# Hybrid encoder layer: strips of eight key columns, token order changed at the bank reads, six second-stage units by seven products

## The chip, the cores and the metric

The kernel runs on one core of a Trainium2 chip. The metric is the device time of one execution in microseconds (us). A core has a matrix engine (TensorE, PE in the profile; PEld are its weight loads), a vector engine (VectorE, DVE), a scalar engine (ScalarE, ACT), GpSimd (POOL) and SyncE (SP), which here issues nearly all DMA transfers. Each engine works through its own queue in order and waits for the others by semaphores. PSUM has eight banks of 512 fp32 words a partition; matmuls write there, DVE and ACT read it.

## The reference

One layer of an encoder trunk over 2048 tokens (a grid of 32 rows by 64 columns) of width 1024, 16 heads of 64, all fp32. With `DEPTH = 1` only the neighbourhood mixer runs:

```
h = rmsnorm(x, norm_0)
q, k, v, gate = split(h @ w_in_0, 4)
s = q.k / 8 + rpb          # 8 rows x 16 columns of keys around each query
o = softmax(s) @ v
x = x + (o * silu(gate)) @ w_out_0
y = rmsnorm(x, norm_f)
```

A query at row r and column c sees the 8 rows and 16 columns of the grid that lie around it, moved inwards at the border.

## The kernel before

**Numbers.** A product of fp32 matrices is made of three matmuls: every operand is split into a high part (`h`, an ACT copy that rounds to fp32r) and a low part (`l`, a DVE subtraction), and h.h, h.l and l.h are added in PSUM. Each split therefore costs one ACT and one DVE instruction.

**Units and stages.** The columns of q, k and gate (g) are made in units of 256 columns (two head pairs `p`); `(k, 0)` to `(k, 3)` are the four units of k. Tokens come in four chunks `c` of 512. `stage_one` (lines 546 to 753) makes chunks 0 and 1 of v and then of all twelve units; `stage_two` (756 to 866) makes chunks 2 and 3 of v and of the units in `units_two`, which are k, q and g of j=0. The nine units that are left are made for chunks 2 and 3 by `projections` (868), matmul by matmul between the attention steps.

**Seven products.** In both stages a unit (256 columns by two chunks) is made by `seven_products` (378), a Strassen-Winograd scheme: 7 block products of 12 matmuls, 84 in all, where `projections` takes 96. For that DVE makes four sums of weight quarters (`sum_`, line 400), ACT and DVE split seven weight forms (393, 394), and the products gather in three banks: products 1 and 2 share one, 6, 7 and 4 one, 5 and 3 one. Between products that share a bank the partial result is read: `keep` (ACT, 418) after product 1, `add` (DVE, 422) after 6 and after 7, `out_` (DVE, 428) after 5, 4 and 3, `evac` (DVE, 313 or 315) after 2. In stage one the results are also multiplied by the tokens' rstd `rb[c]` (POOL, 430). `give` (321) turns a finished tile into what is stored: for k a high and a low part (341, 342), for g a gate by tanh (328, 329), for q the tile itself. It is stored to DRAM some matmuls later by `store` (288), which keeps a list by a clock that counts matmuls.

**Token order of before.** x, k, v and g are in grid order (row, column). q is put into tiles when a bank is read: `tiled` and `blocked` (280, 283) order the 8 rows by 64 columns of a chunk as four blocks C of 8 rows by 16 columns, in runs of 16 words. Attention handles one token block T (8 rows) of a head pair p in two steps, with two blocks C each. The keys of (T, C) are a rectangle of `KEY_ROWS[T]` by `KEY_COLS[C]`: 11 to 15 rows, 24 or 32 columns. For the product with v they are cut by `blocks` (61) into groups of four rows by the full width, 96 or 128 keys, the last one with three rows. v has to have the same order: `evac_v` (365) stores it to `vd`, `copy_v` (942) copies it in DRAM to `vc`, once per (p, C, half), with the four rows beside each other, and `load_v` (932) loads one tile per (p, T, C).

**The attention steps.** The loop at 1337 runs through 64 pairs `i` = (p, T, two blocks C), first all p for T=0, then T=1 and 2, then T=3. A step issues loads and the bias tables of the next block (`begin`; `bias`, POOL, 970), then feeds matmuls of the remaining units, later of the output product, to PE (`feed`: an allowance `amount[i]` of 22 a step, and 19.7 in the last 18), then `normalise(i-1)` (DVE 1004, POOL 1006), `turns(i-2)`, `scores(i)` and `values(i-2)`. `scores` makes s in four banks (988), adds bias and mask while it takes the row maximum (DVE 995), and takes exp (ACT 998). `turns` transposes the weights on PE (1011) and brings them to SBUF, one half of the queries by DVE (1036), the other by ACT (1035, with another instruction for a group of three rows). `values` multiplies by v (1056), and after the second step of a block DVE multiplies by the gate (1070).

**The end of a row.** The output product (1250 to 1254), residual and final norm follow in `outputs`; `finish` (1169) puts the root (eight tiny DVE instructions), the scaling and the store of a tile of 128 rows on the list, 12, 24 and 44 matmuls later.

Of the kernel before, what the change touches and what calls it, by code (L numbers as in the profile page):

```python
# [10 lines left out]
F32 = mybir.dt.float32  # L11
# [12 lines left out]
NP = H // 2  # L24
# [19 lines left out]
def mask_table():  # L44
    out = []
    for t, (u0, u1) in enumerate(TYPE_ROWS):
        T = (0, 1, 3)[t]
        for c, (v0, v1) in enumerate(TYPE_COLS):
            C = (0, 1, 3)[c]
            qr = T * 8 + np.arange(8)[:, None, None, None]  # L50
            qc = C * 16 + np.arange(16)[None, :, None, None]
            kr = T * 8 + np.arange(u0, u1)[None, None, :, None]
            kc = C * 16 + np.arange(v0, v1)[None, None, None, :]
# [17 lines left out]
def build(ctx, tc, x, xr, xt, wg, rpb, w_out, n0, nf, masks, out):  # L71
# [7 lines left out]
    vd = [dram.tile([4, 4, GW, 8, 128], F32, name=f"vd{u}") for u in range(2)]  # L79
    vc = {(p, C): dram.tile([4 * (c1 - c0), 8, 128], F32, name=f"vc{p}_{C}")  # L80
          for p in range(NP) for C, (c0, c1) in enumerate(KEY_COLS)}
# [12 lines left out]
    vp = pool("vp", 4)  # L94
# [114 lines left out]
    def spread_rstd(c):  # L209
        p = bank(512, "prb")  # L210
        h, l = dgs.pop(c)
        nc.tensor.matmul(p, onesr, h, start=True, stop=False)
        nc.tensor.matmul(p, onesr, l, start=False, stop=True)
        rb[c] = rbp([128, 512], F32, "rb")
        nc.scalar.activation(rb[c], p, AF.Copy)
# [5 lines left out]
    units_two = [(k, j) for j in range(1) for k in "kqg"]  # L221
    halves = [(k, j, 1, c) for j in range(1, 4) for g in (("k", "q", "g") if j < 3 else ("k", "qg")) for c in (2, 3) for k in g]
# [57 lines left out]
    def tiled(t):  # L280
        return t.rearrange("p (r C c) -> p C r c", r=8, c=16)

    def blocked(t):
        return t.rearrange("p (C r c) -> p C r c", r=8, c=16)
# [24 lines left out]
    def evac(kind, hp, c, p, then=None):  # L309
        state["event"] = clock[0]  # L310
        tmp = ev([128, 512], F32, "tmp")
        if kind != "q":
            nc.vector.tensor_tensor(tmp, p, rb[c], OP.mult)
        else:
            nc.vector.tensor_tensor(blocked(tmp), tiled(p), tiled(rb[c]), OP.mult)
        if then is None:
            give(kind, hp, c, tmp)
        else:
            then.append(lambda: give(kind, hp, c, tmp))

    def give(kind, hp, c, t, psum=False):
# [3 lines left out]
        written.add((kind, hp, c))  # L325
        if kind == "g":
            sg = ev([128, 512], F32, "sg")
            nc.scalar.activation(sg, t, AF.Tanh, scale=0.5)
            nc.vector.scalar_tensor_tensor(sg, sg, 1.0, t, op0=OP.add, op1=OP.mult)
            store(("g", hp, c), 12, lambda: nc.sync.dma_start(sgd[hp][:, s], sg))  # L330
            return
        if kind == "q":
            if psum:
                o = ev([128, 512], F32, "q")
                nc.scalar.activation(blocked(o), tiled(t), AF.Copy)
                t = o
# [4 lines left out]
        nc.scalar.activation(hi, t, AF.Copy)  # L341
        nc.vector.tensor_tensor(lo, t, hi.bitcast(F32), OP.subtract)
# [22 lines left out]
    def evac_v(u, t, p):  # L365
        v = ev([128, 512], F32, "v")
        nc.scalar.activation(v, p, AF.Copy, scale=rt[:, t:t + 1] if t < 8 else 1.0)
        dst = vd[u].rearrange("h r c g d -> g (r c) h d")[t // 2, t % 2 * 128:t % 2 * 128 + 128]
# [9 lines left out]
    def seven_products(us, c0, X1, also):  # L378
# [37 lines left out]
        def keep(n):  # L416
            U[n, 1] = ep([128, 512], F32, "p1")
            nc.scalar.activation(U[n, 1], B[n, 1], AF.Copy)

        def add(n, i, P):  # L420
            U[n, i] = xp([128, 512], F32, "u")
            nc.vector.tensor_tensor(U[n, i], B[n, P], U[n, 1], OP.add)  # L422

        def out_(n, a, c, P, u, then):
            kind, j = us[n]
            tmp = ev([128, 512], F32, "tmp")
            lay, of = (blocked, tiled) if kind == "q" else (lambda t: t, lambda t: t)
# [968 lines left out]
```

## Time and profile before

| | |
|---|---|
| time, median of 3 runs (lowest to highest) | 1084.95 us (1084.85 to 1085.42) |
| the profiled execution: time / span | 1086.36 us / 1084.5 us |
| busy PE / DVE / ACT / POOL | 1071.1 / 703.2 / 531.2 / 357.9 us |
| granted TensorE clock | 0.999 |
| DMA: bytes, mean rate | 231.90 MB, 214 GB/s |

Lines of the profile are named by the line of kernel.py (L411 is line 411). A busy PE means that some matmul is under way; matmuls overlap, so their durations add up to more than the time that they take. The stages lie at 1.8 to 96.7 us (v of stage one), 96.7 to 326.7 (twelve units), 326.7 to 414.2 (v of stage two), 414.2 to 471.2 (three units), and from there the attention steps, with the tail of the output product from 1028.

### The profile page before, as it was taken

The numbers are of one execution on the slowest core, as the hardware profiler recorded it, in microseconds if no ns is written. First come the engines' busy times: TensorE is split into PE (matmuls) and PEld (weight loads), VectorE is DVE, ScalarE is ACT, GpSimd is POOL, SyncE is SP. The second block draws the span as 40 slices with busy tenths as digits, with TensorE's granted clock in tenths as the row PEclk, the third lists the DMA queues.
The fourth block names the chain that finished last, engine by engine and source line by source line (L and its number), as shares of the span: only waits on it lengthen the run. The fifth ranks groups of instructions, "written<-read, shape, count | busy, mean of one in ns | idle before, by whom it ended". The sixth has DMA issues, their size and how long they took to land.

```text
span 1084.5 us, 21929 instructions
## 1 busy us (share of the span) xinstructions
PE 1071.1 (99%) x7657; PEld 877.1 (81%) x7657; DVE 703.2 (65%) x1644; ACT 531.2 (49%) x1345; POOL 357.9 (33%) x474
## 2 busy tenths in 40 slices
PE   9999999999999999999999999999999999999997
PEld 6888888888888888887888888888888787888885
DVE  5376778778997535576555555664676786776643
ACT  7545334333434334346555555564576565665431
POOL 0000222312221000017545534444447656566200
PEclk9999999999999999999999999999999999999999
DMA  9633557574764366889868876886899787887442
GB/s 313 212 97 106 202 173 210 163 232 146 256 188 143 108 172 170 258 277 310 245 205 267 253 216 204 255 269 200 246 319 294 230 268 231 274 262 226 126 149 78
DMA packets 145901, 231.90 MB, mean 214 GB/s; under 512 B 13824, under 2 KB 61184, under 8 KB 145792
## 3 DMA queue, kind: packets, MB, share of 16 engines
q1 hardware_dynamic: 145648, 230.25, 68.2%
q8 instruction: 61, 1.00, 0.4%
q14 instruction: 48, 0.39, 0.1%
q10 hardware_dynamic: 144, 0.26, 0.1%
HBM read 171.73 MB, written 73.40 MB: 226 GB/s over the span
## 4 chain that ended last, share of the span: by engine, by line
PE 92%; DVE 3%; DMA 1%; ACT 1%; issue 1%; SPq 0%; POOL 0%; ACTq 0%; DVEq 0%; POOLq 0%
PE pp L411 23%; PE pv L531 16%; PE o L1056 8%; PE s L988 6%; PE pp L359 6%; PE pp L357 6%; PE pp L355 6%; PE po L1254 6%; PE po L1252 5%; PE po L1250 5%; PE ph L1011 5%; PE zp L1269 1%; DMA k_hi<-hi 1%; DMA land<-in_xt_dram 0%; DVE f L394 0%
## 5 line engine op out<-in xcount | busy, mean ns | idle before, releaser
L1006 POOL TENSOR_SCALAR x<-x,st 128x360 f32<-128x360 f32 (+5 forms) x256 | 143.0, 578 | 235.0 <-DVE st L1004 192.3
L970 POOL TENSOR_TENSOR em<-e,mk 128x480 f32<-128x480 f32 (+5 forms) x160 | 136.3, 886 | 138.3 <-DMA raw<-in_xt_dram 135.0
L998 ACT ACTIVATE x<-x,st 128x360 f32<-128x360 f32 (+5 forms) x256 | 151.8, 595 | 44.4 <-DVE st L995 44.4
L411 PE MATMUL pp<-h,f 128*128 128x512 f32 x480 | 155.4, 389 | 0.0
L430 POOL TENSOR_TENSOR tmp<-tmp,rb 128x512 f32<-128x512 f32 x36 | 58.9, 1637 | 270.6 <-DVE tmp L428 223.7
L411 PE MATMUL pp<-t,f 128*128 128x512 f32 x540 | 130.0, 390 | 0.3 <-DVE u L422 0.2
L995 DVE CUSTOM_DVE_ANT_0 x<-s,em 128x360 f32<-128x360 f32 (+5 forms) x256 | 124.0, 539 | 5.3 <-PE s L988 1.4
L411 PEld LDWEIGHTS pp<-t,f 128*128 128x128 f32 x540 | 101.2, 188 | 22.2 <-DVE u L422 1.2
L359 PE MATMUL pp<-h,w 128*128 128x512 f32 x288 | 115.1, 400 | 0.0
L357 PE MATMUL pp<-l,w 128*128 128x512 f32 x288 | 113.2, 393 | 0.0
L355 PE MATMUL pp<-h,w 128*128 128x512 f32 x288 | 113.1, 393 | 0.0
L1035 ACT ACTIVATE pta<-ph 96x256 f32<-96x256 f32 (+1 forms) x224 | 58.5, 333 | 104.3 <-PE ph L1011 104.3
L1036 DVE COPY pta<-ph 128x384 f32<-128x384 f32 (+3 forms) x128 | 60.7, 514 | 72.7 <-PE ph L1011 72.5
L411 PEld LDWEIGHTS pp<-h,f 128*128 128x128 f32 x480 | 90.1, 188 | 18.8
L1254 PE MATMUL po<-wol,gh 128*128 128x512 f32 x252 | 100.3, 398 | 0.0
L1252 PE MATMUL po<-woh,gl 128*128 128x512 f32 x252 | 98.9, 393 | 0.0
L1250 PE MATMUL po<-woh,gh 128*128 128x512 f32 x252 | 98.9, 392 | 0.0
L1056 PEld LDWEIGHTS o<-pta,vt 96*64 96x64 f32 (+2 forms) x1792 | 83.6, 137 | 17.2 <-issue 10.2
L1056 PE MATMUL o<-pta,vt 96*64 96x128 f32 (+4 forms) x1792 | 92.3, 254 | 1.4 <-DVE pta L1036 1.0
L411 PE MATMUL pp<-l,f 128*128 128x512 f32 x240 | 93.4, 389 | 0.0
L531 PE MATMUL pv<-wh,h 128*128 128x512 f32 x256 | 88.1, 390 | 0.0
L531 PE MATMUL pv<-wh,l 128*128 128x512 f32 x256 | 88.0, 389 | 0.0
(148 smaller groups left out, 1916.6 us busy)
## 6 DMA issues: line engine op xcount, KB each, us to landing
raw<-in_wg_dram SPq DMA_DIRECT2D x126, 256.0 KB, 5.1
e<-in_rpb_dram SPq DMA_DIRECT2D x54, 240.0 KB, 3.9
vt<-vc SPq DMA_DIRECT2D x64, 192.0 KB, 3.7
row<-in_xr_dram SPq DMA_DIRECT2D x32, 256.0 KB, 4.3
vd<-v SPq DMA_DIRECT2D x32, 256.0 KB, 3.0
k_hi<-hi SPq DMA_DIRECT2D x32, 256.0 KB, 2.6
k_lo<-lo SPq DMA_DIRECT2D x32, 256.0 KB, 3.8
vc<-vd SPq DMA_DIRECT2D x32, 256.0 KB, 4.4
```

What stands on the lines that cost most here:

```text
L355: nc.tensor.matmul(p, wh[w, b][:, cols], hh[k, c], start=(k == 0), stop=False)
L357: nc.tensor.matmul(p, wh[w, b][:, cols], hl[k, c], start=False, stop=False)
L359: nc.tensor.matmul(p, wl[w, b][:, cols], hh[k, c], start=False, stop=(k == NK - 1))
L411: nc.tensor.matmul(B[n, P], t[:, int(m == 2), c], x[k][int(m == 1)], start=P in (1, 6, 5) and k == 0 and m == 0, stop=k == 3 and m == 2, s ...
L531: nc.tensor.matmul(ps[t], a[:, o], b, start=k == 0 and m == 0, stop=k == NK - 1 and m == 2)
L970: (nc.gpsimd if attending[0] or not s else nc.vector).tensor_tensor(sh(t), E[p, s][:, u0 + 4:u1 + 4, v0 + 8:v1 + 8], sh(MK[0][:, m0:m0 + n ...
L998: nc.scalar.activation(X[i, C][s], X[i, C][s], AF.Exp, bias=st[:, s:s + 1], scale=-1.0, accum_out=st[:, 2 + s:3 + s])
L1006: nc.gpsimd.tensor_scalar(X[i, C][s], X[i, C][s], st[:, 4 + s:5 + s], 0.5, op0=OP.mult, op1=OP.mult)
L1056: nc.tensor.matmul(o[s * 64:s * 64 + 64, C * 128 + q0:C * 128 + q0 + nq], vt[C][:k, g - g0_, s * 64:s * 64 + 64], t[:k, at:at + nq], start ...
L1250: nc.tensor.matmul(p, gh, woh[q, j], start=(i == 0), stop=False)
L1252: nc.tensor.matmul(p, gl, woh[q, j], start=False, stop=False)
L1254: nc.tensor.matmul(p, gh, wol[q, j], start=False, stop=(i == NK - 1))
```

## The change

**Strips.** Keys are cut by columns: a strip is 8 columns by all key rows of the block (88, 120 or 96 keys), and `strips(C)` takes the place of `blocks(T)`. A block C has two strips that both halves of its queries see, and one or two that one half sees. Queries are ordered by strip, row, column. k is kept in order (row, column in the strip, strip) until its bank is read; the x that feeds the row statistics and the projections is given to the kernel in that order (the residual x and the output in the order of the queries), so the rows of v come out in it too, and a load of whole token rows of `vd` gives one partition per (row, column in the strip) with all eight strips beside each other. `copy_v` and `vc` go, and `load_v` makes one load per (p, T), into two buffers of 1024 words instead of four of 512.

**Bank reads.** `of` and `lay` change the order in every instruction that reads a bank of q, k or g: `of` reads the bank at a step of 8 words, and `lay` writes in sequence. For chunks 0 and 1 rstd is put into k's order first; stage one makes the four k units first, then q and g, and ACT reorders rstd in between (`reorder_rstd`). The scores read k in runs of 8 words, and `bias` reads the bias and writes in strips.

**Six units.** `units_two` holds k, q and g of j=0 and j=1; six units are left for the attention steps, and the allowance per step becomes 15.5 (8 more in each of the first three steps). The limit to which feeding may run ahead is half the allowance instead of 12.

**Roots.** In place of three entries in the list, finished tiles wait in `roots`, and `run_roots` takes them in the odd steps.

```diff
-def blocks(T):
-    r0, r1 = KEY_ROWS[T]
+def strips(C):
     out = []
-    for g in range(r0 // 4, (r1 + 3) // 4):
-        halves = [h for h in range(2) if abs(2 * T + h - g) <= 1]
-        out.append((g, 4 * g - r0, min(4, r1 - 4 * g), halves[0] * 64, len(halves) * 64))
+    for s in range(KEY_COLS[C][0] // 8, KEY_COLS[C][1] // 8):
+        halves = [h for h in range(2) if abs(2 * C + h - s) <= 1]
+        out.append((s, s - KEY_COLS[C][0] // 8, halves[0] * 64, len(halves) * 64))
     return out
...
+    def reorder_rstd(c):
+        t = rbp([128, 512], F32, "rb")
+        nc.scalar.activation(t.rearrange("p (s r c) -> p s r c", r=8, c=8),
+                             rb[c].rearrange("p (r s c) -> p s r c", s=8, c=8), AF.Copy)
+        rb[c] = t
...
-    units_two = [(k, j) for j in range(1) for k in "kqg"]
+    units_two = [(k, j) for j in range(2) for k in "kqg"]
...
+    def of(kind, t):
+        return t.rearrange("p (r c s) -> p r s c", c=8, s=8) if kind == "k" else t.rearrange("p (n s) -> p s n", s=8)
+
+    def lay(kind, t):
+        return t.rearrange("p (r s c) -> p r s c", s=8, c=8) if kind == "k" else t.rearrange("p (s n) -> p s n", s=8)
...
-        if kind != "q":
-            nc.vector.tensor_tensor(tmp, p, rb[c], OP.mult)
-        else:
-            nc.vector.tensor_tensor(blocked(tmp), tiled(p), tiled(rb[c]), OP.mult)
+        nc.vector.tensor_tensor(lay(kind, tmp), of(kind, p), lay(kind, rb[c]), OP.mult)
...
         def keep(n):
-            nc.scalar.activation(U[n, 1], B[n, 1], AF.Copy)
+            nc.scalar.activation(lay(kind, U[n, 1]), of(kind, B[n, 1]), AF.Copy)
 
         def add(n, i, P):
-            nc.vector.tensor_tensor(U[n, i], B[n, P], U[n, 1], OP.add)
+            nc.vector.tensor_tensor(lay(kind, U[n, i]), of(kind, B[n, P]), lay(kind, U[n, 1]), OP.add)
...
-            nc.vector.tensor_tensor(lay(tmp), of(B[n, P]), of(u), OP.add)
+            nc.vector.tensor_tensor(lay(kind, tmp), of(kind, B[n, P]), lay(kind, u), OP.add)
             if c0 == 0:
-                nc.gpsimd.tensor_tensor(lay(tmp), lay(tmp), of(rb[c]), OP.mult)
+                nc.gpsimd.tensor_tensor(tmp, tmp, rb[c], OP.mult)
...
     def stage_one():
-        us = [(k, j) for j in range(4) for k in "kqg"]
+        us = [("k", j) for j in range(4)] + [(k, j) for j in range(4) for k in "qg"]
...
-            if m and i in (1, 3, 5):
-                copies(0, 1)
+            if (m, i) == (4, 0):
+                reorder_rstd(0)
+                reorder_rstd(1)
...
+    def load_v(p, T):
+        r0, r1 = KEY_ROWS[T]
+        must(*[("v", p // 4, t) for t in range(r0 // 2, (r1 + 1) // 2)])
+        rows = vd[p // 4][p % 4].rearrange("(k s) d -> k s d", s=8)[8 * r0:8 * r1]
+        VT[p, T] = t = vp([128, 1024], F32, "vt").rearrange("p (s d) -> p s d", s=8)
+        nc.sync.dma_start(t[:8 * (r1 - r0)], rows)
...
-                    nc.tensor.matmul(pst[s], qq[a, qs], kk[a, :r1 - r0, c0:c1], start=(m == 0), stop=(m == 2))
+                    nc.tensor.matmul(pst[s], qq[a, qs], kk[a, :r1 - r0, c0:c1].rearrange("p r (s c) -> p s r c", c=8), start=(m == 0), stop=(m == 2))
...
-                if four < len(halves_[h]):
-                    k = halves_[h][four][2] * width(C)
-                    put(slots[:k, h, 2 * four:2 * four + 2],
-                        ph[h][:k, 128 * four:128 * four + 128].rearrange("p (n q) -> p n q", q=64))
+                put(slots[:k, h, :2 * n], ph[h][:k, :128 * n].rearrange("p (n q) -> p n q", q=64))
...
+    def run_roots():
+        while roots and (roots[0][0] <= clock[0] or ended[0]):
+            _, n, root, scale, send = roots.pop(0)
+            root()
+            store(("y", n), 9, scale)
+            store(("y", n), 27, send)
...
     early = 96 * (12 - len(units_two)) + 192
-    amount = [early / 48] * 48 + [(384 - 30) / 18] * 18
+    first = 8
+    amount = [(early - 3 * first) / 48] * 48 + [(384 - 30) / 18] * 18
+    calm_debt = amount[0] / 2
+    for i in range(3):
+        amount[i] += first
...
-        while credit[0] > 0 or credit[0] > -12 and clock[0] - state["event"] < calm:
+        while credit[0] > 0 or credit[0] > -calm_debt and clock[0] - state["event"] < calm:
...
-        if 0 < i <= N:
-            p, T, cs = pairs[i - 1]
-            later_loads(load_v(p, T, cs[0]) + load_v(p, T, cs[1]), 0, 2)
+        if i % 2 == 0 and i < N:
+            load_v(*order[m])
...
         quiet[0] = i % 2 == 1 or i >= N
+        if quiet[0]:
+            run_roots()
```

More of the change, by code (lines that the diff above doesn't have):

```diff
@@ L78, in build @@
     sgd = [dram.tile([128, S], F32, name=f"sgd{p}") for p in range(NP)]
-    vd = [dram.tile([4, 4, GW, 8, 128], F32, name=f"vd{u}") for u in range(2)]
-    vc = {(p, C): dram.tile([4 * (c1 - c0), 8, 128], F32, name=f"vc{p}_{C}")
-          for p in range(NP) for C, (c0, c1) in enumerate(KEY_COLS)}
+    vd = [dram.tile([4, S, 128], F32, name=f"vd{u}") for u in range(2)]
     ogd = [dram.tile([128, 4, NP, 128], F32, name=f"ogd{T}") for T in range(4)]
@@ L93, in build, with vh @@
     qp = pool("qp", 4)
-    vp = pool("vp", 4)
+    vp = pool("vp", 2)
+    vhalf = []
+    def vh(shape, dt, nm):
+        if not vhalf:
+            t = vp([128, 1024], dt, nm)
+            vhalf.extend((t[:, :512], t[:, 512:]))
+        return vhalf.pop(0)
     sp = pool("sp", 2)
@@ L627, in also @@
                     split_v(0, 1, 1)
-                    L2["x12"] = [vp([128, 512], F32, "land") for _ in range(4)]
+                    L2["x12"] = [vh([128, 512], F32, "land") for _ in range(4)]
                     for k in range(4):
@@ L792, in pair @@
                     do[b]()
-                if u and ts != (12,) and b % 2:
-                    copies(1, 1)
         def both(*fs):
@@ L1047, in values @@
         o = O[p, T]
-        g0_ = KEY_ROWS[T][0] // 4
-        vt = {C: VT.pop((p, T, C)) for C in cs}
+        vt = VT[p, T]
         for C in cs:
@@ L1356, in build @@
             values(i - 2)
+    ended[0] = True
+    store(("roots",), 8, run_roots)
     while next(outs, 0) != 0:
```

137 lines of the change are left out of this document (57 added, 80 removed).

## The prediction

> **What bounds the kernel now.** I read the page first: span, busy shares, the chain that ended last.
>
> ```profile
> span 1084.5 us, 21929 instructions
> PE 1071.1 (99%) x7657; PEld 877.1 (81%) x7657; DVE 703.2 (65%) x1644; ACT 531.2 (49%) x1345; POOL 357.9 (33%) x474
> PE 92%; DVE 3%; DMA 1%; ACT 1%; issue 1%; SPq 0%; POOL 0%; ACTq 0%; DVEq 0%; POOLq 0%
> ```
>
> TensorE is busy for 1071.1 of 1084.5 us (its granted clock is 1.00 in the rows below), and 92% of the chain is its own work. So a change is worth the TensorE time that it takes out, as long as no other engine becomes late. Second, the stretches by stage. Columns: window and its length, then busy us (instructions) of PE, PEld, DVE, ACT, POOL, then clock and DMA.
>
> ```profile
> 96.70:326.70 230.00, 229.65 (x1012) 189.51 (x1011) 190.81 (x281) 88.81 (x172) 57.32 (x35) 1.00 0.62 193
> 414.20:471.20 57.00, 57.00 (x253) 47.18 (x253) 33.70 (x52) 17.47 (x32) 3.44 (x4) 1.00 0.81 249
> 499.80:623.50 123.70, 123.70 (x1153) 101.45 (x1149) 65.35 (x218) 68.33 (x215) 65.11 (x106) 1.00 0.81 252
> 623.50:905.40 281.90, 281.00 (x2876) 229.72 (x2877) 181.85 (x518) 166.01 (x485) 145.35 (x200) 1.00 0.80 248
> 905.40:1028.00 122.60, 121.34 (x1175) 99.47 (x1176) 84.77 (x271) 66.47 (x193) 69.33 (x103) 1.00 0.72 229
> ```
>
> They are: the twelve first-stage units by seven products; the three second-stage units; the attention steps of token block T=0 (15 steps, counted by the `o` pieces of the chain), of T=1 and 2 (32), and those at the end. VectorE is the second engine everywhere, and it is nearest to the limit in the first row: 190.81 of 230 us.
>
> Third, what a matmul costs. The table of groups gives a mean near 390 ns, but that is start to end of one in a pipeline. The interval comes from the chain in order of time (start, us, what) and from the timeline of PE between two attention parts (first and last of 23 starts in a row):
>
> ```profile
> 96.72 78.89 PE pp L411 x348
> ```
> ```profile
> 645.26 0.39 PE L355 MATMUL pp<-h,w 128*128 128x512 f32 x1
> ...
> 650.28 0.39 PE L357 MATMUL pp<-l,w 128*128 128x512 f32 x1
> ```
>
> 78.89 / 348 = 0.2267 us in the seven products; (650.28 - 645.26) / 22 = 0.228 us for the matmuls that fill the attention steps. Who takes 0.39 us for a matmul overrates this change by 1.7.
>
> **The change part by part.**
>
> *Three more units by seven products.* k, q and g of j=1 leave the fill of the attention steps: 3 x 96 = 288 matmuls x 0.228 = 65.7 us less there. They join the second stage's products: 3 x 84 = 252 x 0.2267 = 57.1 us more. Net -8.6 us, all on the engine that sets the end. What they bring along on other engines lies under them: the stage-two row has VectorE busy 33.70 of 57.00 us for three units.
>
> *What the shorter attention steps uncover.* The allowance per step falls from 22 matmuls to 15.5 (two thirds of 24 more in the first three steps), so a step loses 6.5 x 0.228 = 1.48 us of cover. T=0: 123.70 / 15 = 8.25 falls to 6.8 us; T=1 and 2: 281.90 / 32 = 8.81 falls to 7.3 us. Busy per step today: T=0 has DVE 4.4, ACT 4.6, POOL 4.3; T=1 and 2 has DVE 5.7, ACT 5.2, POOL 4.5. All fit, and DVE and ACT also lose a third of the fill's weight splits and evictions. The end row, at 19.7 matmuls a step, shows PE idle for 122.60 - 121.34 = 1.3 us only, about a per cent. I take 0 to +1, and +0.2.
>
> *Bank reads in a new order.* Every PSUM read of q, k and g (line 313 or 315, 335, 341, 418, 422, 428) now takes elements 8 words apart. In a first-stage unit that is six VectorE reads (one 313/315, two 422, three 428) and one ScalarE read. The trace shows no such step. Its nearest rows are q's reads in runs of 16 words beside k's contiguous ones, on both engines:
>
> ```profile
> L313 DVE TENSOR_TENSOR tmp<-pp,rb 128x512 f32<-128x512 f32 x8 | 5.5, 688 | 3.7 <-PE pp L411 3.7
> L315 DVE TENSOR_TENSOR tmp<-pp,rb 128x512 f32<-128x512 f32 x4 | 2.8, 688 | 1.2 <-PE pp L411 1.2
> L335 ACT ACTIVATE q<-pp 128x512 f32<-128x512 f32 x13 | 7.8, 599 | 18.1 <-PE pp L359 18.1
> L341 ACT ACTIVATE hi<-pp 128x512 fp32r<-128x512 f32 x13 | 7.7, 591 | 1.6 <-PE pp L359 1.4
> L1036 DVE COPY pta<-ph 128x384 f32<-128x384 f32 x48 | 26.3, 548 | 22.9 <-PE ph L1011 22.9
> L1036 DVE COPY pta<-ph 128x256 f32<-128x256 f32 x16 | 6.7, 417 | 9.2 <-PE ph L1011 9.0
> ```
>
> 688 against 688 ns, and 599 against 591: a hop after 16 words is free. The lower end is 0 for a hop at every element too (nothing in it saves time). For the upper end, an element costs (548 - 417) / 128 = 1.02 ns; an element that took two such turns would add 512 x 1.02 = 0.52 us to each read, 3.1 us to a unit. What that does is read from units of the first stage, 19.1 us each, as DVE stood in them:
>
> ```profile
> 211.30:230.40 19.10, 19.10 (x86) 15.83 (x85) 16.32 (x22) 8.11 (x16) 4.92 (x4) 1.00 0.66 191
> 268.60:287.70 19.10, 18.89 (x83) 15.31 (x82) 18.69 (x26) 7.49 (x14) 5.80 (x4) 1.00 0.82 262
> 287.70:306.80 19.10, 19.10 (x86) 15.79 (x86) 18.19 (x25) 6.37 (x11) 4.29 (x4) 1.00 0.51 172
> 306.80:326.60 19.80, 19.80 (x89) 16.41 (x88) 18.11 (x24) 9.91 (x18) 6.38 (x4) 1.00 0.72 228
> ```
>
> 16.32 becomes 19.4, 0.3 over, and some four units are like it; the last three become 21.8, 21.3 and 21.2, over by 2.7, 2.2 and 1.4. Together about +7.5 us. Little of it can be absorbed: products 6, 7 and 4 accumulate in one bank, so the read after 6 has to be done before 7 starts, one product (12 x 0.2267 = 2.7 us) later. PE's waits (us in total, times, longest) have this one once, at 0.2 us, in the sixth row:
>
> ```profile
> PE zp L1269 <- POOL z L1266: 1.8, 1, 1.8
> PE o L1056 <- DVE pta L1036: 1.0, 3, 0.3
> PE s L988 <- DVE lo L342: 0.9, 1, 0.9
> PE s L988 <- ACT pta L1035: 0.9, 3, 0.4
> PE o L1056 <- ACT pta L1035: 0.3, 1, 0.3
> PE pp L411 <- DVE u L422: 0.2, 1, 0.2
> PE s L988 <- DVE y L1161: 0.2, 1, 0.2
> ```
>
> The second stage has room even then: 33.70 / 3 = 11.2 us of DVE a unit, and at most ten such reads make it 16.4 of 19. Between 0 and +7.5 I take 0, since the rows nearest to it (same engines, same bank, same size, a broken order) show no trace of a cost. This is the weakest step of the sum.
>
> [...]
>
> *k before q and g in stage one; the statistics of two chunks reordered.* A k unit and a g unit both end in four ScalarE and four VectorE instructions more than q. Four k units in a row keep the load of the 16.32 row above, still under 19.1. The two reorder copies are ScalarE, which has 8 of 19 us. Bound 0 to +0.5; I take +0.2.
>
> *Values: one load for a (p, T), no copies.* The page's DMA issues:
>
> ```profile
> vt<-vc SPq DMA_DIRECT2D x64, 192.0 KB, 3.7
> vc<-vd SPq DMA_DIRECT2D x32, 256.0 KB, 4.4
> ```
>
> These are the largest of their groups: 64 copies vd to vc and 128 loads of vt go, 32 loads of 4 KB a partition come, 160 issues fewer on SP's queue and its two DRAM passes gone. The new load waits, as the four did, for the buffer that the values of the step before have just left; behind it on SP stand the keys, the bias rows and the stores of that step, and its reader comes two steps later (13 us, a 192 KB load lands in 3.7 us). No load is among the waits of PE above, so this is worth 0 to -1; I take 0.
>
> *Turns, values, scores.* Strips make 22 transposes a step in place of 20 or 24 and 14 products in place of 12 or 16, the same totals. One eviction per half replaces one or two:
>
> ```profile
> L1035 ACT ACTIVATE pta<-ph 96x128 f32<-96x128 f32 x48 | 13.0, 271 | 0.0
> L988 PE MATMUL s<-kt,qh 64*128 64x360 f32 x128 | 18.0, 346 | 0.0
> L988 PE MATMUL s<-kt,qh 64*128 64x352 f32 x64 | 11.1, 350 | 0.9 <-DVE lo L342 0.9
> L970 POOL TENSOR_TENSOR em<-e,mk 128x360 f32<-128x360 f32 x44 | 40.2, 935 | 0.0
> L970 POOL TENSOR_TENSOR em<-e,mk 128x352 f32<-128x352 f32 x15 | 13.9, 949 | 1.3 <-DVE st L995 1.3
> ```
>
> ScalarE saves 96 such small evictions (these 48, and as many for the outer columns) of 0.27 us and widens others, beside TensorE: 0. Keys and bias are now read in runs of 8 words. 360 columns are 15 rows of 24, 352 are 11 rows of 32: four rows more cost neither PE (346 against 350) nor POOL (935 against 949) anything, so 0.
>
> *Roots in odd steps.* Eight tiny VectorE instructions a tile change their place on an engine that is busy for 84.77 of 122.60 us: 0, at most 0.3 either way.
>
> **Sum.** -8.6 + 0.2 + 0 + 0.2 = -8.2 us. The profiled execution took 1086.36 us (1.86 around its span), so it would take 1078.2; the median of 1084.95 lies 1.41 below that execution, and gives 1076.8, say 1077.
>
> **The rivals.** *A, moderate: the hop costs, the gain is eaten in stage one.* For it: DVE at 18.69 of 19.1 us, and a read that must end within one product. Against it: the equal rows 313 and 315. At +7.5 us 1084.3. [...]
>
> *B, the other side: the hop costs more than two turns.* At 0.75 us a read a unit's DVE work grows by 4.5 us; the ordinary units (16.32) are over by 1.7 four or five times and the last three by 4.1, 3.6 and 2.8, together some 18: 1095. It ends above 1087.1 as soon as a read costs about 0.6 us more.
>
> *C, the attention steps do not shrink by all of their cover.* The chain bias (POOL), scores, exp, reciprocal, POOL, turns runs over two steps, which get 3 us shorter. If a tenth of the 65.7 us stays, 1083.4; past 8.2 / 65.7 = 12.5% the gain is gone. Against it: the busy sums above, and a step of 6.2 us between two score parts that the chain of today passes without a wait:
>
> ```profile
> 576.26 0.91 PE s L988 x10
> 577.17 1.26 PE o L1056 x24
> 582.44 0.99 PE s L988 x9
> ```
>
> *D, scores slow down by short runs.* The chain gives scores 6% of the span, some 65 us; at half speed 1142, and 13% is enough to lose all. Against it: 346 and 350.
>
> ```profile
> PE pp L411 23%; PE pv L531 16%; PE o L1056 8%; PE s L988 6%; PE pp L359 6%; PE pp L357 6%; PE pp L355 6%; PE po L1254 6%; PE po L1252 5%; PE po L1250 5%; PE ph L1011 5%; PE zp L1269 1%; DMA k_hi<-hi 1%; DMA land<-in_xt_dram 0%; DVE f L394 0%
> ```
>
> **How the numbers follow.** About 0.2%, 2.2 us, is what a measurement of this kernel can tell. The forecast has 0.54 with its own range 1075 to 1079; A 0.17 (1079 to 1087), B 0.13, C 0.10 (1079 to 1090), D 0.06. Faster by over 0.2% (below 1082.8): 0.54, 0.07 of A and 0.04 of C, 0.65. Within 0.2%: 0.07 of A and 0.02 of C, 0.09. Slower: 0.03 of A, 0.13, 0.04 of C, 0.06, in all 0.26. The range goes from 1074.5 (-8.6 and the idle that copies may cause) to 1089, where most of B and D, less than 2 in 10, is left out.
>
> **What would show it.** Six units in 6 x 19.0 = 114 us of the second stage; lines 422 and 428 still at 688 ns (A and B: 1.0 to 1.4 us, PE waiting for DVE u or tmp between 100 and 330 us); steps of 6.8 and 7.3 us with PE still at 99% (C: waits of turns for POOL x or of values for pta); scores of 360 columns at 346 ns (D). The forecast is wrong if a bank read grows by half a microsecond, or if PE idles in the attention steps by over 0.1 us a step.

## The result

The changed kernel takes 1088.61 us (median of 9 runs, 1086.12 to 1090.48), the kernel before, in the same session, 1085.36 us (9 runs, 1084.8 to 1086.2). The ratio is 1.0028, with an interval of 1.0018 to 1.0039: 3.25 us slower, where 8 us faster was forecast. Of the changed kernel's nine executions seven had a mean granted clock of 0.995 and took 1088.38 to 1090.48 us, and two had 0.999 and took 1086.12 and 1086.33. The profiled execution took 1090.37 us with a span of 1088.6 us.

First the page of the kernel after: span and busy shares.

```profile
span 1088.6 us, 21531 instructions
PE 1071.1 (98%) x7621; PEld 875.0 (80%) x7621; DVE 724.2 (67%) x1680; ACT 531.8 (49%) x1260; POOL 355.7 (33%) x474
```

PE is busy for 1071.1 us, exactly as before, although 36 matmuls are gone. So time came back elsewhere, as busy time of PE. The chain that ended last breaks off in the tail for this execution; the stages have to be read from the windows (window and length, then busy us and instructions of PE, PEld, DVE, ACT, POOL, then clock and DMA). The stretches answer to those shown of before: twelve units, second stage, T=0, T=1 and 2, the end.

```profile
96.20:326.60 230.40, 230.00 (x1012) 189.39 (x1012) 190.47 (x281) 90.25 (x173) 56.75 (x35) 1.00 0.52 160
414.10:528.40 114.30, 114.30 (x506) 94.66 (x505) 68.13 (x108) 36.82 (x65) 3.33 (x4) 1.00 0.49 155
549.20:660.80 111.60, 110.74 (x1234) 90.47 (x1233) 70.35 (x229) 66.33 (x191) 69.19 (x112) 1.00 0.79 238
660.80:908.50 247.70, 241.79 (x2495) 195.75 (x2496) 169.89 (x501) 151.84 (x405) 147.41 (x206) 0.99 0.77 240
908.50:1032.00 123.50, 122.75 (x1271) 100.34 (x1270) 81.68 (x264) 67.73 (x192) 66.73 (x102) 1.00 0.66 209
```

Stage one takes what it took (230.40 for 230.00 us), with the same VectorE time. The second stage takes 114.30 us for six units. T=0 has 16 steps here (15 in the row of before), 6.98 us each; the 24 extra matmuls of the first steps ran ahead of this row. The fourth row is the bad one: 32 steps in 247.70 us, 7.74 a step. Before it was 281.90 us; less 32 x 1.48 us of cover this should be 234.5. The row is 13.2 us over, PE is idle in it for 5.9 us (before: 0.9), and it is the only one whose clock is below 1.00. Counted from each matmul's start to the next one's, the fill gave up 43.4 us (445 matmuls became 256) and not 47.4, and the score matmuls with their waits grew by 10.4 us, from 45.7 to 56.1.

PE's waits (total us, times, longest):

```profile
PE s L978 <- DVE pta L1019: 2.3, 3, 1.3
PE zp L1261 <- POOL z L1258: 1.9, 1, 1.9
PE s L978 <- DVE y L1140: 1.6, 1, 1.6
PE s L978 <- ACT pta L1018: 1.5, 1, 1.5
PE o L1033 <- DVE pta L1019: 1.2, 2, 0.9
PE s L978 <- DVE lo L350: 0.4, 1, 0.4
PE o L1033 <- ACT pta L1018: 0.3, 1, 0.3
PE pp L419 <- DVE u L432: 0.2, 1, 0.2
```

The waits of the attention steps for turns and residual (rows 1, 3, 4, 5, 7) sum to 6.9 us; the rows of before that name turns or residual sum to 2.4. The third row is no price of the roots: PE waits there at 797.7 us, and the first root starts at 843.8. The wait of the seven products (last row) is the same 0.2 us.

Two places tell more. The first is the score part, from the first score matmul to the first matmul of the values. On PE's timeline (start, us) one such part of T=1 or 2 in the kernel before, in that after, and in the kernel before with one line changed (first experiment):

```profile
721.01 0.69 PE L988 MATMUL s<-kt,qh 64*128 64x480 f32 x4
...
722.34 1.56 PE L1056 MATMUL o<-pta,vt 128*64 128x128 f32 x32
```
```profile
719.83 0.41 PE L978 MATMUL s<-kt,qh 64*128 64x360 f32 x1
...
721.41 1.44 PE L1033 MATMUL o<-pta,vt 120*64 120x128 f32 x28
```
```profile
652.29 0.74 PE L988 MATMUL s<-kt,qh 64*128 64x480 f32 x4
...
653.79 1.56 PE L1056 MATMUL o<-pta,vt 128*64 128x128 f32 x32
```

1.33, 1.58 and 1.50 us for the same twelve matmuls. Over all parts of T=1 and 2 the medians are 1.41 before and 1.59 after: some 5.6 us in 32 steps, about half of the 10.4. For T=0 they are 1.29 and 1.24, no net loss.

The second place is where the clock falls. Windows of the kernel after, columns as above:

```profile
848.00:862.00 14.00, 14.00 (x143) 11.40 (x139) 9.51 (x35) 8.59 (x24) 11.00 (x15) 1.00 0.85 251
862.00:866.00 4.00, 2.49 (x34) 1.87 (x34) 3.83 (x9) 1.64 (x4) 2.35 (x2) 0.96 0.86 342
866.00:872.40 6.40, 5.52 (x38) 4.53 (x35) 4.79 (x14) 2.62 (x8) 5.57 (x9) 0.50 0.25 77
872.40:880.00 7.60, 7.60 (x80) 6.11 (x79) 3.96 (x13) 4.40 (x13) 5.05 (x7) 0.99 0.99 296
```

PE idles for 1.51 of 4 us, and then its granted clock is 0.50 for 6.40 us. PE works for 5.52 of these (the 28 products with v take 2.62 us here, 1.44 in the part shown above), half of which, 2.8 us, is lost, and idles for 0.88 us more. Together that is some 5.2 us, an estimate from these rows. PE's own timeline names the two waits:

```profile
865.27 1.17 PE L978 MATMUL s<-kt,qh 64*128 64x360 f32 x4 [1.51 <-ACT pta L1018]
...
867.63 2.62 PE L1033 MATMUL o<-pta,vt 120*64 120x128 f32 x28 [0.88 <-DVE pta L1019]
```

It waited first for ScalarE's copies of the turns, which hold a bank that the scores need, then for VectorE's. VectorE, ScalarE and GpSimd in the same place:

```profile
859.83 0.21 DVE L1156 TENSOR_SCALAR st<-st 128x1 f32<-128x1 f32 x1
...
861.42 0.21 DVE L1156 TENSOR_SCALAR st<-st 128x1 f32<-128x1 f32 x1
...
862.50 1.15 DVE L1161 SCALAR_TENSOR_TENSOR st<-st 128x1 f32<-128x1 f32 x1
...
864.56 2.42 DVE L1170 SCALAR_TENSOR_TENSOR y<-y,st,acc 128x512 f32<-128x512 f32 x2
866.91 0.21 DVE L994 RECIPROCAL st<-st 128x2 f32<-128x2 f32 x2
867.04 0.99 DVE L1019 COPY pta<-ph 120x384 f32<-120x384 f32 x2
```
```profile
864.12 0.72 ACT L1171 ACTIVATE y<-y,st 128x512 f32<-128x512 f32 x1 [1.86 <-DVE st L1163]
864.75 0.74 ACT L1018 ACTIVATE pta<-ph 120x384 f32<-120x384 f32 x2
```
```profile
862.35 1.28 POOL L1172 TENSOR_TENSOR y<-y,acc 128x512 f32<-128x512 f32 x1 [3.35 <-ACT y L1171]
864.92 1.51 POOL L1172 TENSOR_TENSOR y<-y,acc 128x512 f32<-128x512 f32 x1 [1.30 <-ACT y L1171]
```

`run_roots` finds two finished tiles in this odd step and issues two chains of eight tiny instructions one behind the other. Their scalings follow, and only then the reciprocal and VectorE's copies of the turns: 7.2 us from the first root instruction to those copies. ScalarE is held up too: its scaling of the second tile (L1171) stands in its queue ahead of the copies, and it sat idle for 1.86 us until the second chain had ended. The second tile's root fell beside the first tile's scaling: L1161 of the second chain took 1.15 us where the first chain's took 0.22, began 0.15 us after GpSimd's part of that scaling and ended 0.02 us after it. The second L1170 likewise ended 0.55 us after GpSimd's next one.

### The profile page after: what moved, and what is told of

It is laid out like the page before. It is cut to its first block, busy times and chain, and to the rows that moved or that the text cites. A ratio compares the mean times of both kernels' runs of the same rounds, so it can differ in the third digit from the quotient of the medians.

```text
span 1088.6 us, 21531 instructions
## 1 busy us (share of the span) xinstructions
PE 1071.1 (98%) x7621; PEld 875.0 (80%) x7621; DVE 724.2 (67%) x1680; ACT 531.8 (49%) x1260; POOL 355.7 (33%) x474
## 5 line engine op out<-in xcount | busy, mean ns | idle before, releaser
L419 PE MATMUL pp<-h,f 128*128 128x512 f32 x576 | 186.5, 389 | 0.0
L419 PE MATMUL pp<-t,f 128*128 128x512 f32 x648 | 156.0, 390 | 0.3 <-DVE u L432 0.2
L419 PEld LDWEIGHTS pp<-t,f 128*128 128x128 f32 x648 | 121.5, 188 | 26.4 <-DVE u L432 1.2
L1019 DVE COPY pta<-ph 120x384 f32<-120x384 f32 (+5 forms) x128 | 62.9, 516 | 63.2 <-PE ph L1015 62.6
L1033 PEld LDWEIGHTS o<-pta,vt 120*64 120x64 f32 (+2 forms) x1792 | 84.6, 138 | 19.8 <-issue 15.6
L1018 ACT ACTIVATE pta<-ph 120x384 f32<-120x384 f32 (+5 forms) x128 | 52.3, 459 | 88.5 <-PE ph L1015 88.4
L1033 PE MATMUL o<-pta,vt 120*64 120x128 f32 (+5 forms) x1792 | 93.5, 256 | 1.5 <-DVE pta L1019 1.2
L978 PE MATMUL s<-kt,qh 64*128 64x480 f32 (+5 forms) x512 | 86.8, 379 | 6.0 <-DVE pta L1019 2.3
L540 PE MATMUL pv<-wl,h 128*128 128x512 f32 x256 | 87.9, 389 | 0.0
L402 DVE TENSOR_TENSOR f<-raw,f 128x512 fp32r<-128x512 f32 x90 | 69.9, 776 | 22.4 <-ACT f L401 22.4
```

Of the source, the lines that this page charges most:

```text
L402: nc.vector.tensor_tensor(t[:, 1], src, t[:, 0].bitcast(F32), OP.subtract)
L419: nc.tensor.matmul(B[n, P], t[:, int(m == 2), c], x[k][int(m == 1)], start=P in (1, 6, 5) and k == 0 and m == 0, stop=k == 3 and m == 2, s ...
L540: nc.tensor.matmul(ps[t], a[:, o], b, start=k == 0 and m == 0, stop=k == NK - 1 and m == 2)
L978: nc.tensor.matmul(pst[s], qq[a, qs], kk[a, :r1 - r0, c0:c1].rearrange("p r (s c) -> p s r c", c=8), start=(m == 0), stop=(m == 2))
L1033: nc.tensor.matmul(o[s * 64:s * 64 + 64, C * 128 + q0:C * 128 + q0 + nq], vt[:k, strip, s * 64:s * 64 + 64], t[:k, at:at + nq], start=firs ...
```

## The experiments

Times are medians; each ratio is against the kernel before, run in the same call (its medians there: 1085.33 to 1085.85 us).

**1. The score matmuls' runs of 8 alone, in the kernel before.**

```diff
-kk[a, :r1 - r0, c0:c1], start=(m == 0)
+kk[a, :r1 - r0, c0:c1].rearrange("p r (s c) -> p s r c", c=8), start=(m == 0)
```

> The kernel before, with one edit: the score matmuls read the keys of a rectangle strip by strip, in runs of 8 words, instead of row by row in runs of 24 or 32 (the scores of a row then stand in another order than bias and values, so the output is not the reference's; the work is the same). Theory S, the short runs cost matmul time: the time from the first score matmul to the first values matmul of a T=1 or 2 step goes from 1.34 to 1.42 us to about 1.6 us, and the kernel from 1085.4 to about 1091 to 1092 us. Rival E, the longer score part of the changed kernel comes from the evictions of the turned weights for which the values wait: that part stays at 1.34 to 1.42 us and the time at 1085.4 us.

1091.16 us, ratio 1.0052 (1.0037 to 1.0067): 5.7 us for nothing but the order in which PE reads keys from SBUF. PE's busy time grew by as much, from 1071.1 to 1076.9 us. (Experiments 1 to 3 leave out the order of bias and values that would fit these scores; the work is the same.) A score matmul with 480 columns (15 rows of 32) goes from 382 to 417 ns from start to end; in order the groups of before, of this kernel, of the next one, and of the kernel after:

```profile
L988 PE MATMUL s<-kt,ql 64*128 64x480 f32 x64 | 13.8, 382 | 0.0
```
```profile
L988 PE MATMUL s<-kt,ql 64*128 64x480 f32 x64 | 14.9, 417 | 0.0
```
```profile
L988 PE MATMUL s<-kt,ql 64*128 64x480 f32 x64 | 14.6, 426 | 0.0
```
```profile
L978 PE MATMUL s<-kt,ql 64*128 64x480 f32 x64 | 17.7, 414 | 0.0
```

**2. Runs of 4 in the kernel before** (one execution).

```diff
-kk[a, :r1 - r0, c0:c1], start=(m == 0)
+kk[a, :r1 - r0, c0:c1].rearrange("p r (s c) -> p s r c", c=4), start=(m == 0)
```

> The same edit with runs of 4 words (output again not the reference's). If a run costs something of its own, the cost doubles against runs of 8: score part about 1.8 us in T=1 and 2 steps. If only the break of a row order costs, it is as with runs of 8, about 1.6 us. By rival E it stays at 1.34 to 1.42 us.

1094.68 us, 9.2 over before. So the cost grows with the number of runs, but not in proportion: three to four times as many runs (8 words) cost 5.7, six to eight times as many cost 9.2.

**3. The long runs put back into the kernel after.**

```diff
-kk[a, :r1 - r0, c0:c1].rearrange("p r (s c) -> p s r c", c=8), start=(m == 0)
+kk[a, :r1 - r0, c0:c1], start=(m == 0)
```

> The changed kernel, with one edit: the score matmuls read the keys row by row in runs of 24 or 32 words again (the order of scores does not fit bias and values any more, so the output is not the reference's; the work is the same). Theory S: the score part of T=1 and 2 steps falls from 1.58 us to about 1.4 us, and the time by 6 to 7 us, from 1088.6 to about 1082 us. Rival E: 1.58 us and 1088.6 us stay.

1083.11 us, 0.9983 (0.9972 to 0.9993), 5.5 less than the kernel after. The same price from the other side. It settles rival D's mechanism, at a small size, and leaves some 6 us of the miss open: at 1083.11 the gain is 2 us, not 8.

**4. The roots back on the list**, as before, 12, 24 and 44 matmuls after the tile.

```diff
-        if ended[0]:
-            store(("y", n), 12, root)
-            store(("y", n), 24, scale)
-            store(("y", n), 44, send)
-        else:
-            roots.append((clock[0] + 8, n, root, scale, send))
+        store(("y", n), 12, root)
+        store(("y", n), 24, scale)
+        store(("y", n), 44, send)
```

> The changed kernel, with root, scaling and store of each output tile put on the list 12, 24 and 44 matmuls later again, as the kernel before does. Theory R, two roots and their scalings in one odd step make VectorE late for the evictions of the turned weights: the waits of PE at 863 to 868 us (1.5 and 0.9 us) and at 900 us (1.3 us) go, the granted clock stays at 0.999 in all runs, and the time falls by 3 to 5 us to about 1084 us. Rival L, the shorter cover of the steps makes VectorE late whatever the order of the roots: the waits come back at these or other steps and the time stays within 1 us of 1088.6 us.

1086.33 us, 1.0013 (1.0000 to 1.0026), but its twelve runs fall apart: eight from 1083.66 to 1086.78 at a mean clock of 0.997 to 0.999, four from 1089.6 to 1090.94 at 0.994 to 0.996. It points to the roots and doesn't settle what about them costs: on the list they only move to other places among the same shortened steps.

**5. Three units in the second stage instead of six**, all else as after; the allowance is then 21.5.

```diff
-    units_two = [(k, j) for j in range(2) for k in "kqg"]
-    halves = [(k, j, 1, c) for j in range(2, 4) for g in (("k", "q", "g") if j == 2 else ("k", "qg")) for c in (2, 3) for k in g]
+    units_two = [(k, j) for j in range(1) for k in "kqg"]
+    halves = [(k, j, 1, c) for j in range(1, 4) for g in (("k", "q", "g") if j < 3 else ("k", "qg")) for c in (2, 3) for k in g]
```

> The changed kernel with three second-stage units by seven products again (j=0 alone) and nine in the attention steps, whose allowance is then 21.5 matmuls. Theory C, the six units save their 8.7 us of matmul time and lose most of it because steps with output work and little fill make PE wait: the time becomes about 1090 us, 1 to 3 us above the changed kernel, with no wait of PE over 1 us and none in the clock. Rival N, the waits come from strips and roots and not from the allowance: they stay, and the time becomes 1088.6 + 8.7, about 1097 us.

1091.62 us, 1.0055 (1.0041 to 1.0069). The waits of PE did not go away with the long steps; the stretch behind its own pair of roots (860.2 and 861.8 us):

```profile
864.00:872.00 8.00, 6.89 (x67) 5.19 (x67) 7.06 (x19) 4.46 (x12) 5.29 (x7) 0.87 0.42 132
```

So short steps are not the sole cause of the stalls, and the six units do bring time: 3 us in this comparison.

**6. Less cover early, more where the residual and the roots begin.**

```diff
-    amount = [(early - 3 * first) / 48] * 48 + [(384 - 30) / 18] * 18
+    amount = [13.0] * 36 + [(early - 3 * first - 36 * 13.0) / 12] * 12 + [(384 - 30) / 18] * 18
```

> The changed kernel, with the same 768 matmuls of the first 48 steps shared out otherwise: 13 a step in the first 36 (21 in the first three, as 8 more there stay), 23 in the 12 after them, in which the last units end and the output product begins. Theory C: the long score parts at 795, 813 and 863 us and the stretch at half clock go, and the time falls by 4 to 6 us to about 1083 us. Rival N: the waits come at the same steps (counted by number) and the time stays within 1 us of 1088.6. A third outcome, if 13 matmuls do not cover the earlier steps: new waits between 550 and 790 us, time above 1088.

1086.99 us, 1.0012 (1.0003 to 1.0021): 1.6 less than after. Cover in the right place buys a part of the stalls.

**7. k stored by strips**, so that a score matmul reads one contiguous run. All three kinds then use the same bank order, rstd is not reordered, and the stores and loads of k carry the order (views at 64 and 120 words).

```diff
-        return t.rearrange("p (r c s) -> p r s c", c=8, s=8) if kind == "k" else t.rearrange("p (n s) -> p s n", s=8)
+        return t.rearrange("p (n s) -> p s n", s=8)
...
+    def keyed(t):
+        return t.rearrange("p (s m) -> p s m", s=8)
...
-        store(("k", hp, c), 12, lambda: (nc.sync.dma_start(k_hi[hp][:, s], hi.bitcast(F32)),
+        store(("k", hp, c), 12, lambda: (nc.sync.dma_start(keyed(k_hi[hp])[:, :, c * 64:c * 64 + 64], keyed(hi.bitcast(F32))),
...
-            nc.sync.dma_start(t[:, :n].bitcast(F32), src[p][:, r0 * GW:r1 * GW])
+            nc.sync.dma_start(keyed(t[:, :n].bitcast(F32)), keyed(src[p])[:, :, r0 * 8:r1 * 8])
...
-kk[a, :r1 - r0, c0:c1].rearrange("p r (s c) -> p s r c", c=8), start=(m == 0)
+kk[a, c0 // 8:c1 // 8], start=(m == 0)
```

> The changed kernel, with k in the order strip, row, column from the bank on: stored to DRAM in runs of 64 words, loaded in runs of 88 to 120, and read by the score matmuls in one run; the bank read steps by 8 words over 64 elements as for q, and rstd needs no reordering. Theory S: score parts of T=1 and 2 steps fall from 1.59 us to 1.45 us or less, the time by 4 to 6 us to about 1083 us. If the short pieces in DRAM slow the transfers so far that keys come late, waits for kt appear and the time stays or rises.

1083.36 us, 0.9985 (0.9972 to 0.9997): 5.25 less than after. The 480-column group falls below that of before:

```profile
L978 PE MATMUL s<-kt,ql 64*128 64x480 f32 x64 | 16.2, 375 | 0.0
```

**8. Experiments 4, 6 and 7 together.**

```diff
+        store(("y", n), 12, root)
...
+    amount = [13.0] * 36 + [(early - 3 * first - 36 * 13.0) / 12] * 12 + [(384 - 30) / 18] * 18
...
+kk[a, c0 // 8:c1 // 8], start=(m == 0)
```

> The changed kernel with keys by strip, the allowance of 13 and 23, and the roots on the list as before. If S, C and R each take their part: about 1077 us, the time that the saved matmuls alone give. If one cause is behind two of them: 1080 to 1083 us.

1078.95 us, 0.9940 (0.9928 to 0.9952): it beats both kernels, 6.9 us under before in its call.

**9. Three units, and the roots on the list** (edits of 5 and 4).

```diff
-    units_two = [(k, j) for j in range(2) for k in "kqg"]
+    units_two = [(k, j) for j in range(1) for k in "kqg"]
...
+        store(("y", n), 12, root)
```

> The changed kernel with three units by seven products (allowance 21.5) and the roots on the list as before: of the change only strips, bank reads and loads are left. Theory R, with two roots in one odd step as the cause of the waits that stood at 803, 823 and 867 us even with 21.5 matmuls a step: the score parts there fall under 2 us and the time goes from 1091.6 to about 1089, which leaves about the price of the short runs (4 to 6 us) over the kernel before. Rival: the evictions of turned weights or the bias on GpSimd make those waits; they stay, 1091.6.

1090.47 us, 1.0041 (1.0028 to 1.0054), 1.2 less than with three units alone; the intervals overlap, and waits of the score parts of 2 to 3 us stayed where they were. That the place of the roots made the stalls is not confirmed by this run.

**10. At most one root in an odd step of the kernel after.**

```diff
             store(("y", n), 27, send)
+            if not ended[0]:
+                break
```

> The changed kernel, with at most one tile's root in an odd step. Theory R2, it is the pair of roots with their scalings in one step that makes VectorE late: the waits at 863 to 868 us and at 900 us go, and the time falls from 1088.6 to that of the roots on the list, about 1086 us. Rival: it is the odd step that is the wrong place, with one root as with two: 1088 to 1089 us.

1083.75 us (10 runs, 1083.33 to 1084.44), 0.9980 (0.9972 to 0.9989): 4.9 less than after, by two lines. VectorE's timeline in the place where two roots stood in a row:

```profile
858.71 0.21 DVE L1156 TENSOR_SCALAR st<-st 128x1 f32<-128x1 f32 x1
...
861.01 0.75 DVE L1170 SCALAR_TENSOR_TENSOR y<-y,st,acc 128x512 f32<-128x512 f32 x1
861.68 0.22 DVE L994 RECIPROCAL st<-st 128x2 f32<-128x2 f32 x2
861.81 1.00 DVE L1019 COPY pta<-ph 120x384 f32<-120x384 f32 x2
```

3.1 us from the first root instruction to the copies, where it was 7.2. PE has no gap there and the clock stays at 1.00:

```profile
856.00:864.00 8.00, 8.00 (x104) 6.54 (x103) 7.68 (x29) 5.78 (x15) 4.69 (x8) 1.00 1.00 355
864.00:872.00 8.00, 8.00 (x93) 6.54 (x89) 5.46 (x21) 5.25 (x17) 8.00 (x11) 1.00 0.91 255
```

The score matmuls of this step begin at 862.67 us in the profiled kernel after and at 861.57 here, those of the next step at 875.71 and 868.99: of the 6.1 us between the two spans (1088.6 and 1082.5) 5.6 arise in this place. So it is two roots in one step that cost, not their being in odd steps. PE's waits for turns and residual still sum to 4.0 us (after: 6.9, before: 2.4).

**11. Keys by strip and roots on the list** (edits of 7 and 4), without the moved cover.

```diff
+        store(("y", n), 12, root)
...
+kk[a, c0 // 8:c1 // 8], start=(m == 0)
```

> Keys by strip and roots on the list, with the changed kernel's even allowance of 15.5. If the allowance of 13 and 23 was what took the last waits away: about 1081 us, 2 us above the kernel with all three. If its price in the T=0 steps (score parts of 2.8, 3.2 and 1.9 us) was as large as its gain: about 1079.

1079.08 us, 0.9934 (0.9920 to 0.9949). Against 1078.95 with the cover moved, the difference is within the noise: no gain from the moved cover is seen once the other two are mended.

**12. The same, with 14.5 matmuls for 36 steps and 18.5 for 12.**

```diff
-    amount = [(early - 3 * first) / 48] * 48 + [(384 - 30) / 18] * 18
+    amount = [14.5] * 36 + [(early - 3 * first - 36 * 14.5) / 12] * 12 + [(384 - 30) / 18] * 18
```

> Keys by strip, roots on the list, 14.5 matmuls a step in the first 36 and 18.5 in the next 12. If the T=0 waits come of too little cover there: they shrink, no score part over 2.5 us is left after the start, and the time is 1077 to 1078 us. If the late steps need 23: waits at 795 to 870 us come back, 1080 to 1081 us.

A miss: 1085.23 us (1083.43 to 1088.79), 0.9999 (0.9989 to 1.0008), although its allowance lies between those of experiments 8 and 11. Its profile has two stretches with a low clock:

```profile
548.00:558.00 10.00, 8.07 (x71) 6.55 (x70) 5.31 (x18) 6.02 (x18) 8.93 (x14) 0.69 0.93 218
818.00:832.00 14.00, 11.77 (x96) 9.26 (x97) 7.78 (x17) 4.86 (x14) 6.83 (x11) 0.76 0.71 193
```

PE idles for 1.93 and 2.23 us in them. In the second, its wait of 2.23 us is for VectorE's copies of the turns, which stand behind a split of an output weight (L184) that took 3.19 us instead of 0.69. Why this allowance lines up work that the two beside it do not was not settled.

**13. Keys by strip and one root a step** (edits of 7 and 10).

```diff
+            if not ended[0]:
+                break
...
+kk[a, c0 // 8:c1 // 8], start=(m == 0)
```

> The changed kernel with keys by strip and at most one root in an odd step; the even allowance of 15.5 stays. If short runs and paired roots are two separate losses, their repairs add up: 1083.8 - 5.3 = about 1078.5 us. If the faster score part brings new waits of values for evictions: 1080 to 1083 us.

1079.59 us, 0.9945 (0.9932 to 0.9957). 1088.61 less 5.25 less 4.86 is 1078.5: the two losses are separate and add up, within an uncertainty of some 2 us. Its page:

```profile
span 1077.8 us, 21533 instructions
PE 1062.5 (99%) x7621; PEld 868.8 (81%) x7621; DVE 718.8 (67%) x1680; ACT 530.6 (49%) x1258; POOL 356.8 (33%) x474
```

PE's busy time falls by 8.6 us against both kernels.

**14. Three units and one root a step** (edits of 5 and 10).

```diff
-    units_two = [(k, j) for j in range(2) for k in "kqg"]
+    units_two = [(k, j) for j in range(1) for k in "kqg"]
...
+            if not ended[0]:
+                break
```

> The changed kernel with three units by seven products (allowance 21.5) and at most one root in an odd step. Theory F, with the pair of roots gone the six units give their full matmul time: this is 8 to 9 us above the 1083.8 us of the kernel with six units and one root, about 1092 us. Theory C, the shorter cover takes a good part of the gain by itself: only 4 to 6 us above it, 1088 to 1090 us.

1089.61 us, 1.0039 (1.0024 to 1.0054). Against experiment 10, each measured from the before of its own call (+4.28 and -2.05), the three further units are worth 6.3 us once the roots don't interfere, with an uncertainty of some 2 us.

## Why the prediction was wrong

Point by point, in its own order.

*Three more units by seven products, -8.6: right as PE time.* The second stage came to 114.30 us where 114 was named. By the intervals of all matmuls, the seven products grew from 286.6 to 343.8 us and the fill of the attention steps fell from 204.9 to 139.0: -8.7.

*Bank reads, 0: right.* This was called the weakest step, and it held. The groups of the kernel after, with the step of 8 words, DVE and ACT:

```profile
L437 DVE TENSOR_TENSOR tmp<-pp,u 128x512 f32<-128x512 f32 x36 | 24.8, 688 | 23.8 <-PE pp L419 23.8
L326 DVE TENSOR_TENSOR tmp<-pp,rb 128x512 f32<-128x512 f32 x12 | 8.3, 690 | 5.7 <-PE pp L419 5.7
L344 ACT ACTIVATE q<-pp 128x512 f32<-128x512 f32 x10 | 5.9, 592 | 7.6 <-PE pp L367 7.6
L349 ACT ACTIVATE hi<-pp 128x512 fp32r<-128x512 f32 x10 | 5.9, 588 | 3.0 <-PE pp L367 2.9
```

688 and 690 ns against 688, 592 against 599, 588 against 591: in these reads an element at every eighth word cost these engines nothing. Rivals A and B fall: no run shows the longer reads that they count with (1.0 to 1.4 us), nor a cost that would give A's lower end of 1079 us.

*Values, turns, k first, +0.2 together: no loss seen.* Experiment 14 is the kernel before with all of these, the short runs and single roots in odd steps; it stands at 1.0039, experiment 1, with the short runs alone, at 1.0052. What is left for the rest is -1.4 us with an uncertainty of about 2. The steps of T=0 bear it out: 6.98 us where 6.8 was forecast, and by the strips each has four products with v more than before (28 for 24), some 0.2 us, as 28 of them take 1.44. T=1 and 2 have four fewer.

*"Keys and bias are now read in runs of 8 words ... so 0": wrong, some 5.3 us.* Three runs give 5.7 (1), 5.5 (3) and 5.25 (7, which also changes how k is stored and loaded). The rows were right and the reading was not: 346 against 350 ns compared 15 runs with 11, a difference of four. The change cuts 15 runs into 45 (360 columns) or 60 (480), some ten times that difference. And it is a mean over overlapping matmuls, about which the prediction itself had warned for the seven products. The 360 columns, which were to stay at 346 ns, took 370 in experiment 1 and 374 in the kernel after:

```profile
L978 PE MATMUL s<-kt,qh 64*128 64x360 f32 x128 | 22.4, 374 | 1.5 <-ACT pta L1018 1.5
```

Rival D named this mechanism, at .06, and priced it at half speed and at the 13% that would lose all; at the measured size it is 5.3 us of the 86.5 that all score matmuls of the kernel before take, 6%, not enough to lose all alone.

*"Roots in odd steps ... 0, at most 0.3 either way": wrong, some 4.9 us.* The term counted instructions and the busy share of the engine (84.77 of 122.60 us), and forgot that `run_roots` empties its list. The prediction looked at the end of the kernel, where cover is long; the loss is in T=1 and 2. What costs is not the eight instructions but what is queued behind two chains of them and their scalings: reciprocal and VectorE's copies of the turns, 4.1 us later, and ScalarE's copies, with PE out of work. Experiment 10 shows it; the same two lines bring 3.8 us with keys by strip (13 against 7) and 2.0 with three units (14 against 5). The two stalls and the half clock, 1.51 + 0.88 + 2.8 us, are about as large as the difference measured. The two executions that kept 0.999 lie some 2.5 us above experiment 10, which suggests that about half of the loss comes by the clock; no trace of these two was kept.

*Shorter steps, +0.2 in bounds of 0 to +1: too small.* Units worth 8.7 us of PE time gave 6.3 in experiment 14, so about 2.4 went to lost cover, rival C at a size of 2.4 / 65.7 = 4%. It fits that experiment 10 has 1.6 us more of PE's waits than the kernel before. This is the least certain of the three, with its uncertainty of 2 us.

The sum: -8.7 + 5.3 + 4.9 + 2.4 = +3.9, measured +3.25. If every run is taken against the kernel before of its own call, short runs cost 5.7 and roots 5.3, and the sum is +4.7; both lie within the uncertainty of some 2 us. The prediction's structure, matmul time out, small costs back in, was right; two terms put at 0 were 10 us together. Short runs cost as much under full cover (experiment 1); the pair of roots fell into steps whose cover had just been cut.

## What to carry to other kernels

When an operand of a matmul is to be read in shorter runs, compare rows that differ by as many runs as the change adds, and measure the interval of the matmuls, not their mean duration; reorder where it is free (here when a bank is read: 688 and 690 ns against 688) so that the matmul sees contiguous words. Work that is deferred into slots needs a limit per slot: two bursts on an engine with idle time (VectorE, busy for 67% of the span) delay the instructions behind them by their sum, and here by more (7.2 us from the first root instruction to the copies, 3.1 with one root), as the second fell beside the work that the first had handed to another engine. On a kernel bound by PE, price a stall of PE at more than its length, since the clock may fall behind it (here to 0.50 for 6.40 us after 1.51 us of idle); and after mending a loss, remeasure the others alone, since the same edit (the cover of 6) was worth 1.6 us or nothing, depending on the rest.

## What was not expected of the hardware

- Runs of the moving operand: a 480-column score matmul took 375 ns contiguous, 382 in runs of 32, 414 to 417 in runs of 8 and 426 in runs of 4 words; for the kernel 5.7 us for runs of 8, 9.2 for runs of 4.
- The clock: after 1.51 us of idle within 4 us it was granted at 0.50 for 6.40 us. In these 4 us PE was busy for the other 2.49.
- Tiny VectorE instructions don't always have their price: L1161 took 0.22 us in the first of the two root chains and 1.15 us in the second, and the two scalings (L1170) 2.42 us together where one took 0.75 in experiment 10. The trace of the kernel after has 43 VectorE instructions that took over 0.3 us longer than the middle one of their line and shape. Every one of them read two operands from SBUF, overlapped GpSimd's work, and ended 0.02 us (128x1) or 0.55 us (128x512) after a GpSimd instruction. Copies from PSUM (L1019) that began beside GpSimd's work kept their time within 0.03 us. The longest was L184, 3.84 us instead of 0.69 beside six bias instructions of 5.52 us, just ahead of PE's wait at 797.7 us. No run here moved GpSimd's work away, so this is read from the traces alone.
